# Layer 1's gate with stationary weights, rounded centred sums in linear attention, and a later second pass

## The chip, the cores and the metric

The kernel runs on one core of one Trainium2 chip. The metric is the device time of one launch in microseconds (us). The core has five engines that run their own instruction streams in order: PE (matrix multiplication; its weight loads are shown apart as PEld), DVE, ACT, POOL and SP. They wait for each other by semaphores. Data lies in on-chip SBUF (128 partitions), PE writes into PSUM (8 banks of 128 x 512 f32), and DMA moves data to and from DRAM. Instructions are named as the profile names them: line of the kernel, engine, operation, output tile <- input tiles.

## The reference

The program is a two-layer backbone over 2048 latent tokens and 256 context tokens of width 1024, both of which go through the layers as 18 row tiles of 128 tokens (tiles 0 and 1 are the context). Layer 0 mixes latent attention (8 heads) and bidirectional gated linear attention (4 heads); layer 1 is neighbourhood attention with 16 heads. What the change touches:

```python
# layer 0, gated linear attention: g = log_sigmoid(logits) / 16, forward and backward
b = jnp.cumsum(gi, axis=-2)                       # within a chunk
q_t, k_t = qi * jnp.exp(b), ki * jnp.exp(-b)
o = einsum(q_t, state) + einsum(tril(q_t k_t), vi)
state = state * jnp.exp(b_last) + einsum(ki * jnp.exp(b_last - b), vi)
b = rms_norm(ol_f + flip(ol_b), gla_gain) * silu(zb)
...
# layer 1
q, k, v, z = jnp.split(jnp.dot(h, w_in), 4, axis=-1)      # 1024 columns each
o = neighborhood_attention(rms_norm(q), rms_norm(k), v, k_ctx, v_ctx, rpb)
y = jnp.dot(o * jax.nn.silu(z), w_out)                    # z of the 2048 latent tokens only
```

## The kernel before

**Products.** A projection is made as three matmuls on rounded operands (type f32r): high x high, high x low, low x high, where high is the rounded value and low the rounded rest (`mm3_steps`, L124 to L131). Other products, the sums of `front` and the transposes among them, take plain f32 operands.

**Stages.** `even_latent` and `even_rest` project layer 0. In `even_rest` the gate of latent attention is already projected with the weights stationary: `pair_steps` (L182 to L194) takes 128 columns of weights as the stationary operand and two row tiles (2 x 128 tokens) as the moving one, 256 columns wide, and so gets the gate transposed. `even_mix` runs latent attention (L936 to L1072: 296 steps of two 512-wide score products, two exponentials on ACT and two additions on DVE, L1041) and weaves linear attention (`gla`, L724 to L915) and the splitting of the output weights between its steps. `odd_qk` projects q and k of layer 1; `odd_vz` projects its v (weight blocks 4 and 5) and gate z (blocks 6 and 7) and weaves in the maxima of the attention scores (`maxes`, L1447 to L1502); `odd_attention` does the attention and the output projection.

**Order.** A timeline model at build time fixes the order of the instructions of each engine. `weave` (L133) takes 0.57 steps of `maxes` for each step of the projections; the stream of cells (`stream`, L196) keeps the modulated input of two row tiles in two slots (`ring`, high and low parts) and reloads a slot (`reload`, L372: a 512 KB load into `x`, a rounding on ACT to `hhi`, a subtraction on DVE L380 to `hlo`) when the last cell of its row tile is done.

**Layer 1's gate before.** A cell (row tile t, block j) is 24 matmuls of 512 columns with the input stationary (L129 to L131). For j = 6 and 7 the gate is formed on ACT (tanh) and DVE (L1389), then turned by four f32 transposes on PE (L1429; L1331 for the two cells that `odd_qk` does), copied out of PSUM by ACT and stored to `z1` in runs of 128 tokens.

**Linear attention before.** `front` (L751 to L783) makes the log gates `gG` of one row tile and sums them along the tokens with two f32 matmuls against triangular matrices of 0 and +-1 (L773). `back` makes the products within the tile. `scan` carries the states over the 18 tiles: forwards on POOL, backwards on DVE (L861 to L863). `second` then goes over the tiles again (`enter` L878: add the state's part, L883, square on ACT L885, sum on DVE L887; `leave` L891: normalise, gate, transpose, store). The hook at L1096 takes one step of the second pass or of the weights at every fourth attention step, from the 166th.

Of the kernel before, what the change touches and what calls it, by code (L numbers as in the profile page):

```python
# [17 lines left out]
P = 128  # L18
# [70 lines left out]
class Kern:  # L89
# [634 lines left out]
    def gla(self, gp, gs, g1, gd, pp, tag):  # L724
# [14 lines left out]
        nc.sync.dma_start(tri[:], self.i["tri"])  # L739
        gn = self.tl(gp, [P, 4], "gn")  # L740
# [10 lines left out]
        def front(c):  # L751
# [15 lines left out]
            G = self.tl(g1, [P, 512], "gG", bufs=1)  # L767
            nc.vector.scalar_tensor_tensor(out=G[:], in0=lg[:], scalar=0.0, in1=e[:], op0=ALU.min, op1=ALU.subtract)
            G4 = G[:].rearrange("p (h z d) -> p h z d", z=2, h=H)
            yield  # L770
            mid = bank()
            for z in range(2):
                nc.tensor.matmul(mid[:].rearrange("p (h z d) -> p h z d", z=2, h=H)[:, :, z, :], tri[:, z, :], G4[:, :, z, :], start=True, stop=True)  # L773
            nc.sync.dma_start(self.gE[c, :, 2], G[0::127])
# [103 lines left out]
        def enter(c, qT, oi, zb):  # L878
# [6 lines left out]
            self.act(sq[:], oi[:], AF.Square)  # L885
            ss = self.tl(gs, [P, H], "gss")
            nc.vector.tensor_reduce(out=ss[:], in_=sq[:].rearrange("p (h t) -> p h t", h=H), axis=AX.X, op=ALU.add)  # L887
# [192 lines left out]
    def even_mix(self, e1, win, hT):  # L1080
# [3 lines left out]
        with ExitStack() as es:  # L1084
            with ExitStack() as esa:
# [190 lines left out]
    def odd_qk(self, ws, win, hT):  # L1276
# [7 lines left out]
        with ExitStack() as es:  # L1284
# [7 lines left out]

            def cell(t, j):
                hi, lo = hT[t]
# [4 lines left out]
                for n, _ in enumerate(steps):  # L1299
                    if n == 5 and pend and (len(pend) > 1 or j in (4, 6)):  # L1300
                        fin(*pend.pop(0))
# [4 lines left out]
                if j == 4:  # L1306
# [3 lines left out]
                    return  # L1310
                if j == 6:
                    n = self.tl(sp, [P, 512], "onat", bufs=4)
                    self.gate(n, ps[:].rearrange("p h d -> p (h d)"))
                    self.marks["a"] = self.last_tanh
                    pend.append((t, j, n))
# [11 lines left out]
            def fin(t, j, n):  # L1327
# [5 lines left out]
                if j == 6:  # L1333
                    self.act(hi[:].bitcast(F32), ps[:])
                    nc.gpsimd.dma_start(self.z1[:4, :, (t - NCT) * P : (t - NCT) * P + P].rearrange("j p t -> p j t"), hi[:].bitcast(F32))
                    return
# [40 lines left out]
            cells += [(t, j) for j in (0, 1, 2, 3, 6, 4) for t in (NT - 2, NT - 1)]  # L1377
# [25 lines left out]

    def odd_vz(self, ws, win, hT):
# [3 lines left out]
        with ExitStack() as es:  # L1408
# [6 lines left out]
            def cell(t, j):  # L1415
                hi, lo = hT[t]
                wh, wl = win[j]
                ps = self.tl(pp, [P, 512], "gm")
                yield from self.mm3_steps(ps[:], (lambda k: hi[:, k, :], lambda k: lo[:, k, :]),
                                          (lambda k: wh[:, k, :], lambda k: wl[k][:]), range(KD))  # L1420
                n = self.tl(sp, [P, 512], "ovz", bufs=3)
                if j < 6:
                    self.act(n[:], ps[:])
                    self.store_v(t, j - 4, n)
                    return
                self.gate(n, ps[:])
                pt = self.tl(pp, [P, 4, P], "tp", bufs=1)
                for i in range(4):
                    nc.tensor.transpose(pt[:, i, :], n[:, i * P : i * P + P], self.ident[:])  # L1429
# [3 lines left out]
                (nc.scalar if t >= NCT + 4 else nc.gpsimd).dma_start(self.z1[(j - 6) * 4 : (j - 6) * 4 + 4, :, o : o + P].rearrange("j p t -> p j t"), z[:])  # L1433
# [482 lines left out]
```

## Time and profile before

| | |
|---|---|
| median of 3 runs | 3614.03 us (3608.65 to 3618.55) |
| the profiled execution, its own time | 3613.5 us |
| its span in the trace | 3611.7 us (1.8 us lie around it) |
| instructions in the span | 52299 |
| mean granted clock of PE | 0.987 |
| linear attention: first load (L755), last normalisation (L894) | 1088.7 us, 1831.0 us |
| transposes of the gate in `odd_vz` (L1429): first, last | 2578.4 us, 3009.6 us |

The page gives the busy time of each engine and its share of the span. The windows view gives the same for stretches of time, with the granted clock of PE (1.00 is full) in the column PEclk. The timeline lists instructions by start and duration; a matmul's duration includes its passage through the array, so what a matmul costs PE is read from the distance between two starts. Waits are listed as who waited for whom, with the total, the number and the longest.

### The profile page before, as it was taken

Reading aid. Unit: us, or ns where it says so; the run is one execution under the profiler, and the core shown is the slowest. Engines: PE = TensorE matmul, PEld = TensorE weight load, DVE = VectorE, ACT = ScalarE, POOL = GpSimd, SP = SyncE. Lnnn points to the kernel's source line nnn. Section 1 sums busy time; section 2 is a strip of 40 time slices with the busy share of each in tenths; the row PEclk is TensorE's granted clock in tenths of the full one; section 3 lists DMA queues with packets and bytes.
Section 4 is the critical chain, followed back from the end, with each engine's and each line's share of the span. In section 5 each row is a group of like instructions: output and inputs, shape, how many; then the busy total and the mean of one; then the engine's idle time right before and its main releaser. Section 6 shows DMA issues by size and latency. Waiting matters only on the chain. (4 is left out here: it accounts for less than half of the span.)

```text
span 3611.7 us, 52299 instructions
## 1 busy us (share of the span) xinstructions
PE 3522.7 (98%) x18620; PEld 2751.5 (76%) x18620; DVE 2375.7 (66%) x4876; ACT 1420.3 (39%) x2687; POOL 1210.8 (34%) x1342
## 2 busy tenths in 40 slices
PE   8999999999999999999999999999999999999899
PEld 6888998999986666656657888888788886555577
DVE  4677666888876776697664345455587874777821
ACT  4544551111115555555652134444422222555510
POOL 1433431101011222212312233333444444767743
PEclk9999999999999999999999999999999998999999
DMA  7555463222243342425524554456644438788654
GB/s 253 148 153 161 141 192 110 78 76 89 67 127 74 90 114 66 121 67 145 156 83 146 169 163 129 142 149 193 206 139 124 134 123 206 210 212 218 183 178 153
DMA packets 396687, 513.67 MB, mean 142 GB/s; under 512 B 61230, under 2 KB 275198, under 8 KB 390523
## 3 DMA queue, kind: packets, MB, share of 16 engines
q1 hardware_dynamic: 353242, 418.68, 40.6%
q0 software_dynamic: 20192, 56.97, 5.4%
q10 hardware_dynamic: 22992, 34.68, 2.9%
q8 instruction: 148, 2.42, 0.3%
q14 instruction: 113, 0.92, 0.1%
HBM read 330.61 MB, written 179.59 MB: 141 GB/s over the span
## 5 line engine op out<-in xcount | busy, mean ns | idle before, releaser
L1041 DVE TENSOR_TENSOR acc<-acc,apt 128x512 f32<-128x512 f32 x512 | 377.1, 765 | 150.4 <-ACT apt L106 146.6
L106 ACT ACTIVATE apt<-st 128x512 f32<-128x512 f32 (+1 forms) x592 | 342.9, 593 | 267.2 <-PE st L1052 222.7
L700 DVE TENSOR_REDUCE mm<-mx 128x1 f32<-128x512 f32 (+1 forms) x656 | 390.7, 629 | 81.5 <-PE mx L699 74.6
L992 PE MATMUL av<-apt,av 128*64 128x512 f32 (+1 forms) x1184 | 269.2, 592 | 0.0
L1050 PE MATMUL st<-aq,akh 97*128 97x512 f32 x576 | 246.1, 427 | 0.2 <-ACT apt L106 0.2
L699 PE MATMUL mx<-mk,mq 96*128 96x512 f32 (+1 forms) x656 | 242.7, 372 | 0.0
L106 ACT ACTIVATE u<-gm 128x352 f32<-128x352 f32 (+1 forms) x144 | 70.4, 496 | 436.1 <-PE gm L131 213.9
L1051 PE MATMUL st<-aq,akh 96*128 96x512 f32 x576 | 228.3, 396 | 0.0
L1052 PE MATMUL st<-aq,akl 96*128 96x512 f32 x576 | 227.9, 396 | 0.0
L1484 DVE CUSTOM_DVE_ANT_1 mx<-mx,mtab 128x465 f32<-128x465 f32 (+14 forms) x576 | 184.3, 338 | 48.6 <-PE mx L1478 35.9
L106 ACT ACTIVATE opt<-opt 128x930 f32<-128x930 f32 (+9 forms) x144 | 119.0, 829 | 240.0 <-POOL opt L1782 138.8
L992 PEld LDWEIGHTS av<-apt,av 128*64 128x64 f32 x1184 | 79.8, 136 | 152.1 <-issue 150.0
L1742 DVE TENSOR_TENSOR opt<-st,tab 128x64 f32<-128x64 f32 (+10 forms) x576 | 142.9, 316 | 76.2 <-PE st L1582 46.0
L1617 POOL TENSOR_TENSOR oacc<-oacc,opt 128x682 f32<-128x682 f32 (+9 forms) x144 | 172.6, 1219 | 35.6 <-ACT opt L106 34.2
L1050 PEld LDWEIGHTS st<-aq,akh 97*128 97x128 f32 x576 | 108.6, 188 | 72.4 <-issue 43.4
L1052 PEld LDWEIGHTS st<-aq,akl 96*128 96x128 f32 x576 | 109.7, 190 | 25.2
L699 PEld LDWEIGHTS mx<-mk,mq 96*128 96x128 f32 x656 | 123.7, 189 | 6.0
L1051 PEld LDWEIGHTS st<-aq,akh 96*128 96x128 f32 x576 | 110.2, 191 | 17.6
L106 ACT ACTIVATE x<-px,modB,modA 128x128 f32<-128x128 f32 x272 | 99.1, 468 | 58.4 <-PE px L355 42.6
L1581 PE MATMUL st<-q,kt 128*128 128x480 f32 (+5 forms) x256 | 100.3, 396 | 19.0 <-DVE opt L1742 14.1
L129 PE MATMUL gm<-w0h,hhi 128*128 128x512 f32 x288 | 116.2, 403 | 2.3 <-DVE hhi L367 2.3
L129 PE MATMUL gm<-w1h,hhi 128*128 128x512 f32 x288 | 116.5, 404 | 0.0
(581 smaller groups left out, 10043.8 us busy)
## 6 DMA issues: line engine op xcount, KB each, us to landing
q<-Q SPq DMA_DIRECT2D x48, 512.0 KB
H<-x ACTq DMA_DIRECT2D x36, 512.0 KB
adaw<-ada_w SPq DMA_DIRECT2D x64, 256.0 KB
x<-H SPq DMA_DIRECT2D x32, 512.0 KB
K1t<-okt POOLq DMA_DIRECT2D x32, 512.0 KB, 6.8
kt<-K1t SPq DMA_DIRECT2D x32, 512.0 KB
mtab<-rpb_q SPq DMA_DIRECT2D x16, 899.0 KB
QT<-qkhl SPq DMA_DIRECT2D x36, 384.0 KB
```

Source lines behind the costliest of these rows:

```text
L106: return self.nc.scalar.activation(out, in_, func, **kw)
L129: self.nc.tensor.matmul(out, lh(k), rh(k), start=j == 0, stop=False)
L699: mm = nc.tensor.matmul(ps[:, :w], q[:A_QK, (t % 6) * P : (t % 6) * P + P], k[:A_QK, k0 : k0 + w], start=True, stop=True)
L700: nc.vector.tensor_reduce(out=m[:, t, n : n + 1], in_=ps[:, :w], axis=AX.X, op=ALU.max)
L992: nc.tensor.matmul(O[j, nb][i * 64 : i * 64 + 64, :w], V[j, kt // TT][:, kt % TT, i * 64 : i * 64 + 64], pts[i][:, :w], start=n == 0, stop ...
L1041: self.add = nc.vector.tensor_tensor(out=acc[i][:, :w], in0=a[:, :w], in1=pts[i][:, :w], op=ALU.add)
L1050: nc.tensor.matmul(ps[:, :w], kh[: A_QK + 1, i, kq], qh[: A_QK + 1, :w], start=True, stop=False)
L1051: nc.tensor.matmul(ps[:, :w], kh[:A_QK, i, kq], ql[:A_QK, :w], start=False, stop=False)
L1052: mm = nc.tensor.matmul(ps[:, :w], kl[:A_QK, i, kq], qh[:A_QK, :w], start=False, stop=True)
L1484: nc.vector.tensor_tensor_reduce(out=s, in0=s, in1=tb[:, ri : ri + rn, ci : ci + cn], scale=1.0, scalar=-3e38, op0=ALU.add, op1=ALU.max, a ...
L1617: self.psum = nc.gpsimd.tensor_tensor(out=a, in0=a, in1=pts[:, :, a0 - r0 : a1 - r0, :], op=ALU.add)
L1742: nc.vector.tensor_tensor(out=pt[:, d[0], d[1]], in0=ps[:, d[0], d[1]], in1=tabs[j][i][:, ri : ri + rn, ci : ci + cn], op=ALU.add)
```

## The change

1. `front`: the log gates are written to `e` (f32), rounded by ACT to `gG` (f32r), and the rest `e - gG` goes to a second f32r tile on DVE. The triangular matrices are rounded once into `trr` (0 and +-1 stay what they are). Each of the two f32 matmuls becomes two f32r matmuls (on `gG` and on the rest) that add up in PSUM. The end rows of the log gates are stored from `e`.
2. `enter`: the square on ACT and the sum on DVE become four DVE operations that multiply and sum, one for each head (each is followed by a read of the accumulator).
3. The hook starts at the 174th attention step instead of the 166th.
4. The gate of layer 1: blocks 6 and 7 go through `pair_steps` with two row tiles, in `odd_vz` and for the last two tiles in `odd_qk`. Transposes, their PSUM tile `tp` in `odd_vz` and the copies out of it go; a gate tile is stored in runs of 256 tokens from POOL's queue (`store_z`). The bank of `tp` goes to `mx` (6 instead of 5). The cells of `odd_vz` are in a new order: the gate cells of a pair of tiles (t, t+1) stand between the v cells of t+1 and those of t.

```diff
+        trr = self.tl(gp, [P, 2, P], "trr", F32R, bufs=1)
+        self.act(trr[:], tri[:, :2, :])
...
-            G = self.tl(g1, [P, 512], "gG", bufs=1)
-            nc.vector.scalar_tensor_tensor(out=G[:], in0=lg[:], scalar=0.0, in1=e[:], op0=ALU.min, op1=ALU.subtract)
-            G4 = G[:].rearrange("p (h z d) -> p h z d", z=2, h=H)
+            nc.vector.scalar_tensor_tensor(out=e[:], in0=lg[:], scalar=0.0, in1=e[:], op0=ALU.min, op1=ALU.subtract)
+            nc.sync.dma_start(self.gE[c, :, 2], e[0::127])
+            G = self.tl(g1, [P, 512], "gG", F32R, bufs=1)
+            self.act(G[:], e[:])
+            L = self.tl(gs, [P, 512], "ge", F32R)
+            nc.vector.tensor_tensor(out=L[:], in0=e[:], in1=G[:], op=ALU.subtract)
+            G4, L4 = z4(G[:]), z4(L[:])
             yield
             mid = bank()
             for z in range(2):
-                nc.tensor.matmul(mid[:].rearrange("p (h z d) -> p h z d", z=2, h=H)[:, :, z, :], tri[:, z, :], G4[:, :, z, :], start=True, stop=True)
-            nc.sync.dma_start(self.gE[c, :, 2], G[0::127])
+                nc.tensor.matmul(z4(mid[:])[:, :, z, :], trr[:, z, :], G4[:, :, z, :], start=True, stop=False)
+                nc.tensor.matmul(z4(mid[:])[:, :, z, :], trr[:, z, :], L4[:, :, z, :], start=False, stop=True)
...
-            self.act(sq[:], oi[:], AF.Square)
             ss = self.tl(gs, [P, H], "gss")
-            nc.vector.tensor_reduce(out=ss[:], in_=sq[:].rearrange("p (h t) -> p h t", h=H), axis=AX.X, op=ALU.add)
+            for h in range(H):
+                o = slice(h * P, h * P + P)
+                nc.vector.tensor_tensor_reduce(out=sq[:, o], in0=oi[:, o], in1=oi[:, o], scale=1.0, scalar=0.0,
+                                               op0=ALU.mult, op1=ALU.add, accum_out=ss[:, h : h + 1])
...
-                    if count[0] >= 166 and count[0] % 4 == 2:
+                    if count[0] >= 174 and count[0] % 4 == 2:
...
+            def gated(t, j):
+                wh, wl = win[j]
+                for b in (0, 2):
+                    ps = self.tl(pp, [P, 512], "gm", bufs=3)
+                    for n, _ in enumerate(self.pair_steps(ps, b, (lambda k: wh[:, k, :], lambda k: wl[k][:]))):
+                        if n == 4 and pend:
+                            fin(*pend.pop(0))
+                        if n % 4 == 1 and out_k:
+                            with self.tc.issue_after(self.power.ins):
+                                out_k.pop(0)()
+                        yield
+                    n = self.tl(sp, [P, 512], "onat", bufs=4)
+                    self.gate(n, ps[:])
+                    self.marks["a"] = self.last_tanh
+                    self.store_z(t, (j - 6) * 4 + b, n)
...
-                            pc = self.tl(pp, [P, 2, CTX], "mx", bufs=5)
+                            pc = self.tl(pp, [P, 2, CTX], "mx", bufs=6)
...
+    def store_z(self, t, b, n):
+
+        o = (min(t) - NCT) * P
+        self.nc.gpsimd.dma_start(self.z1[b : b + 2, :, o : o + 256].rearrange("j p t -> p j t"), n[:].rearrange("p (j t) -> p j t", j=2))
...
             def cell(t, j):
+                wh, wl = win[j]
+                w = lambda k: wh[:, k, :], lambda k: wl[k][:]
+                if j > 5:
+                    for b in (0, 2):
+                        ps = self.tl(pp, [P, 512], "gm")
+                        yield from self.pair_steps(ps, b, w)
+                        n = self.tl(sp, [P, 512], "ovz", bufs=3)
+                        self.gate(n, ps[:])
+                        self.store_z(t, (j - 6) * 4 + b, n)
+                    return
...
-                self.gate(n, ps[:])
-                pt = self.tl(pp, [P, 4, P], "tp", bufs=1)
-                for i in range(4):
-                    nc.tensor.transpose(pt[:, i, :], n[:, i * P : i * P + P], self.ident[:])
-                z = self.tl(sp, [P, 4, P], "ozt", bufs=1)
-                self.act(z[:], pt[:])
-                o = (t - NCT) * P
-                (nc.scalar if t >= NCT + 4 else nc.gpsimd).dma_start(self.z1[(j - 6) * 4 : (j - 6) * 4 + 4, :, o : o + P].rearrange("j p t -> p j t"), z[:])
...
-            cells = [(t, j) for j in (7, 5) for t in (NT - 1, NT - 2)]
-            cells += self.cells(list(range(NT))[::-1], (4, 5, 6, 7), lambda t, j: j < 6 or t >= NCT)[8:]
+            cells = [((NT - 1, NT - 2), 7), (NT - 1, 5), (NT - 2, 5)]
+            for t in range(NT - 4, 0, -2):
+                cells += [(t + 1, 4), (t + 1, 5), ((t, t + 1), 6), ((t, t + 1), 7), (t, 4), (t, 5)]
+            cells += [(t, j) for j in (4, 5) for t in (1, 0)]
```

**How the order moves.** PE, the last gate cell before the v cells of the first pair in `odd_vz` (`gm` is the cell's PSUM bank, `w3h` and `w3l` the high and low weights of block 7, `hhi` and `hlo` the input). Before:

```order
L129 MATMUL gm_23572<-w3h_23015,hhi_18332 128x512
L130 MATMUL gm_23572<-w3l_4542_23181,hhi_18332 128x512
L131 MATMUL gm_23572<-w3h_23015,hlo_18333 128x512
L1429 MATMUL tp_23564<-ident_58,ovz_23561 128x128 x4
L129 MATMUL gm_23642<-w1h_23277,hhi_18332 128x512
L130 MATMUL gm_23642<-w1l_4575_23337,hhi_18332 128x512
```

With the change, the same block, where its first pair of 128-column pieces ends and the second begins:

```order
L190 MATMUL gm_23657<-hhi_18460,w3h_23143 128x256
L191 MATMUL gm_23657<-hlo_18461,w3h_23143 128x256
L192 MATMUL gm_23657<-hhi_18460,w3l_4561_23309 128x256
L190 MATMUL gm_23751<-hhi_18460,w3h_23143 128x256
L191 MATMUL gm_23751<-hlo_18461,w3h_23143 128x256
L192 MATMUL gm_23751<-hhi_18460,w3l_4537_23205 128x256
```

The four transposes are gone from between the cells, and the matmuls are half as wide and twice as many.

PE, the sums of the fifth row tile in `front` (`st` is a bank of attention scores, `aq`, `akh` and `akl` their operands, `gl` the bank of linear attention). Before:

```order
L1052 MATMUL st_13197<-aq_13035,akl_10772 128x512
L756 MATMUL gl_11137<-ident_58,gu_1907_11138 96x128
L773 MATMUL gl_11143<-gG_11096,tri_10787 128x4x64 x2
L1050 MATMUL st_13203<-aq_13035,akh_1773_10750 128x512
L1051 MATMUL st_13203<-aq_13035,akh_1773_10750 128x512
```

With the change:

```order
L1060 MATMUL st_13353<-aq_13127,akl_10777 128x512
L779 MATMUL gl_11169<-gG_11120,trr_10789 128x4x64
L780 MATMUL gl_11169<-ge_11122,trr_10789 128x4x64
L779 MATMUL gl_11169<-gG_11120,trr_10789 128x4x64
L780 MATMUL gl_11169<-ge_11122,trr_10789 128x4x64
L822 MATMUL gl_11184<-gqT_11142,gkT_11143 128x128
L1058 MATMUL st_13359<-aq_13127,akh_1774_10751 128x512
```

Two f32 matmuls have become four f32r ones. The whole first pass stands about three attention steps later on PE, and the second pass eight.

DVE, one tile of the second pass. Before (`goi` is the tile's output, `gss` its sums of squares, `acc` the attention's sums):

```order
L883 TENSOR_TENSOR goi_15842<-gl_15929,goi_15842 128x512
L1041 TENSOR_TENSOR acc_3093_15649<-acc_3093_15649,apt_15971 128x512
L887 TENSOR_REDUCE gss_15937<-ge_15935 128x4
L1041 TENSOR_TENSOR acc_3092_15648<-acc_3092_15648,apt_15979 128x512
L1041 TENSOR_TENSOR acc_3093_15649<-acc_3093_15649,apt_15985 128x512
```

With the change:

```order
L889 TENSOR_TENSOR goi_15949<-gl_15953,goi_15949 128x512
L894 ISA ge_15959,gss_15960<-goi_15949 128x128
L894 ISA gss_15960 128x1
L894 ISA ge_15959,gss_15960<-goi_15949 128x128
L894 ISA gss_15960 128x1
L894 ISA ge_15959,gss_15960<-goi_15949 128x128
L894 ISA gss_15960 128x1
L894 ISA ge_15959,gss_15960<-goi_15949 128x128
L894 ISA gss_15960 128x1
L1049 TENSOR_TENSOR acc_3105_15728<-acc_3105_15728,apt_15977 128x512
```

Eight instructions (four products with sums, four reads of the accumulator) stand where one reduction stood, and the attention's addition comes after them.

Up to the first sums of `front`, and from the output projection of layer 0 through `odd_qk` up to its gate cells, the instructions of PE stand in the same order before and after.

More of the change, by code (lines that the diff above doesn't have):

```diff
@@ L1291, in odd_qk @@
             pend, kt, out_k = [], {}, []
+            def gated(t, j):
[13 more added lines that the diff above has]
+                    self.store_z(t, (j - 6) * 4 + b, n)
             def cell(t, j):
+                if j == 6:
+                    yield from gated(t, j)
+                    return
                 hi, lo = hT[t]
@@ L1299, in cell @@
                 for n, _ in enumerate(steps):
-                    if n == 5 and pend and (len(pend) > 1 or j in (4, 6)):
+                    if n == 5 and pend and (len(pend) > 1 or j == 4):
                         fin(*pend.pop(0))
@@ L1309, in cell @@
                     self.store_v(t, 0, n)
[L1310 to L1315, printed above, removed]
                     return
@@ L1376, in odd_qk @@
             cells = self.cells(list(range(NT)), (2, 3, 0, 1), lambda t, j: j > 1 or t >= NCT)[:-8]
-            cells += [(t, j) for j in (0, 1, 2, 3, 6, 4) for t in (NT - 2, NT - 1)]
+            for j in (0, 1, 2, 3, 6, 4):
+                cells += [((NT - 2, NT - 1), j)] if j == 6 else [(t, j) for t in (NT - 2, NT - 1)]
             for _ in self.stream(cells, hT, cell, lambda t: self.prep(1, t, self.x1, pp, ("px", 2)), done):
```

19 lines of the change are left out of this document (6 added, 13 removed).

## The prediction

> **What bounds the kernel now.** I read the page first: the busy shares of the engines and the chain that ended last.
>
> ```profile
> PE 3522.7 (98%) x18620; PEld 2751.5 (76%) x18620; DVE 2375.7 (66%) x4876; ACT 1420.3 (39%) x2687; POOL 1210.8 (34%) x1342
> PE 41%; DVE 2%; DMA 1%; issue 1%; ACT 1%; POOL 0%; SPq 0%; POOLq 0%; DVEq 0%; ACTq 0%
> ```
>
> PE is busy for 98% of the span, no other engine for more than 66%, and of the part of the chain that could be followed PE has by far the most. A share over the whole span hides stages with another limit, so the windows view comes next, for the first pass of linear attention, the end of its scan, its second pass, and `odd_vz`.
>
> ```profile
> core 0: us, PE busy (x) PEld busy (x) DVE busy (x) ACT busy (x) POOL busy (x), PEclk, DMA share, GB/s
> 1070.00:1550.00 480.00, 474.72 (x2428) 303.71 (x2427) 333.53 (x470) 271.81 (x519) 121.79 (x124) 1.00 0.37 94
> 1550.00:1630.00 80.00, 76.51 (x335) 44.59 (x334) 76.21 (x113) 39.42 (x67) 6.68 (x5) 0.98 0.26 72
> 1640.00:1840.00 200.00, 200.00 (x975) 126.49 (x975) 139.46 (x219) 123.23 (x261) 60.52 (x59) 1.00 0.53 149
> 2570.00:3010.00 440.00, 431.70 (x2104) 360.61 (x2103) 335.25 (x1362) 113.08 (x187) 187.85 (x162) 0.99 0.43 134
> ```
>
> PE is the limit in all four. DVE comes close in one: 76.2 of 80 us at the end of the scan, where PE loses 3.5 us. The waits of PE, in 1070 to 1900 us (first row) and in 2540 to 3060 us (the others), are few:
>
> ```profile
> PE gl L825 <- DVE gat L821: 3.5, 1, 3.5
> ...
> PE mx L1478 <- DVE mm L1473: 3.2, 2, 3.0
> PE mx L1471 <- DMA mk<-K: 2.0, 1, 2.0
> PE mx L1478 <- DVE mm L1484: 1.6, 2, 1.0
> PE tp L1429 <- DVE ovz L1389: 1.4, 1, 1.4
> ```
>
> So the time is set by what PE is given to do, and the change is costed as PE work, with the other engines as a check.
>
> **Transposes removed.** The timeline of PE near the end of `odd_vz` shows a run of 512-column matmuls and then one group of four transposes.
>
> ```profile
> 3000.46 0.40 PE L129 MATMUL gm<-w3h,hhi 128*128 128x512 f32 x1
> ...
> 3002.77 0.39 PE L130 MATMUL gm<-w3l,hhi 128*128 128x512 f32 x1
> 3003.00 0.60 PE L1429 MATMUL tp<-ident,ovz 128*128 128x128 f32 x4
> 3003.35 0.48 PE L131 MATMUL gm<-w3h,hlo 128*128 128x512 f32 x1
> 3003.67 0.40 PE L129 MATMUL gm<-w0h,hhi 128*128 128x512 f32 x1
> ```
>
> From 3000.46 to 3002.77 there are ten starts: 0.231 us for one matmul of 512 columns. From 3002.77 to 3003.67 PE did two of these (0.462) and the group: 0.90 - 0.462 = 0.44 us for the group, the slow first matmul behind it included. The number of groups:
>
> ```profile
> L1429 PE MATMUL tp<-ident,ovz x120: 270/272/328, 2578.4 to 3009.6; 128*128 128x128 f32 x120
> ```
>
> That is 30 groups, and the two gate cells of `odd_qk` have one each. 32 x 0.44 = **14.1 us less**.
>
> **Matmuls of half the width.** Two cells of 24 matmuls x 512 columns become 96 x 256. The gate in `even_rest` already runs in this form:
>
> ```profile
> L190 PEld LDWEIGHTS gm<-hhi,WUh x288: 187/190/193, 545.0 to 1063.8; 128*128 128x128 f32 x144
> 545.21 0.28 PE L190 MATMUL gm<-hhi,WUh 128*128 128x256 f32 x1
> ...
> 556.21 0.28 PE L190 MATMUL gm<-hhi,WUh 128*128 128x256 f32 x1
> ```
>
> Between the two starts lie 93 matmuls: 11.00 / 93 = 0.1183 us each. A pair of cells costs 96 x 0.1183 = 11.36 us against 48 x 0.231 = 11.09, so 0.27 more, and 16 pairs (16 row tiles, two blocks) **4.3 us more**. The weight loads last 0.19 us each, longer than the distance of the matmuls, and are hidden all the same, since successive ones overlap. In the Trainium skill, "TensorE: Matmul & The Clock Gate" (part 1, on the measured gap) a warm matmul has a fixed cost of about 2.5 ns beside its columns. By that figure the 768 additional matmuls would cost 1.9 us, as an estimate. The rows here decide: they give 4.3 us.
>
> **Sums of `front`.** One row tile of the first pass:
>
> ```profile
> 1183.53 0.40 PE L1052 MATMUL st<-aq,akl 96*128 96x512 f32 x1
> 1183.77 1.03 PE L773 MATMUL gl<-gG,tri 128*128 128x256 f32 x4
> 1184.44 0.58 PE L1050 MATMUL st<-aq,akh 97*128 97x512 f32 x1
> 1184.87 0.40 PE L1051 MATMUL st<-aq,akh 96*128 96x512 f32 x1
> ```
>
> The two f32 products (four records) take 0.67 us, and the next matmul 0.43 instead of 0.23 to 0.24. From 1183.77 to 1184.87 is 1.10 us with one matmul in it. After the change four rounded matmuls of 256 columns and that one take 4 x 0.118 + 0.235 = 0.71. The difference is 0.39 us, x 18 tiles **7.0 us less**. The trace has no rounded matmul whose columns come in pieces of 64; the bounds are 0.20 x 18 = 3.6 us (0.67 - 0.47, the slow successor stays, as where an f32 product follows) and 9 us (0.03 us more for each weight load that then runs ahead); I take 7.0, which the rows give directly.
>
> The sum on PE: -14.1 + 4.3 - 7.0 = **-16.8 us**.
>
> **What goes to other engines.**
>
> ```profile
> L768 DVE SCALAR_TENSOR_TENSOR gG<-gl,ge 128x512 f32<-128x512 f32 x18 | 12.3, 686 | 3.5 <-ACT ge L106 3.3
> L887 DVE TENSOR_REDUCE gss<-ge x18: 677/680/686, 1641.6 to 1828.2; 128x4 f32<-128x512 f32 x18
> L1484 DVE DVE_READ_ACCUMULATOR2_ANT mm<- 128x1 f32 x576 | 82.4, 144 | 0.0
> L1484 DVE CUSTOM_DVE_ANT_1 mx<-mx,mtab 128x120 f32<-128x120 f32 x32 | 9.4, 294 | 0.3 <-PE mx L1478 0.3
> L106 ACT ACTIVATE ovz<-gm 128x512 f32<-128x512 f32 x62 | 36.8, 594 | 113.7 <-PE gm L131 98.5 <-DVE mm L1473 6.1 <-DVE mm L1484 4.8
> ```
>
> In `front` DVE gets a subtraction of the size of L768, 0.69 x 18 = 12.3 us, and ACT a copy of 0.59 x 18 = 10.7. DVE goes from 333.5 to 346 of 480 us; PE hides it. The chain from the log gate to its sums grows by 0.69 + 0.59 = 1.3 us, and the order gives the first pass some three attention steps for it. In `enter` DVE loses 0.68 and gets four times 0.294 + 0.144, together 1.75: +1.07 x 18 = 19.3 us, so that DVE is busy 159 of 200 us instead of 139.5, still under PE. ACT loses 18 squares, and in the gate 32 copies of 0.594. All of this I cost at nothing. Without PE's cover it would be up to 12.3 + 19.3 = 31.6 us. Queued behind the four sums on DVE are the attention's additions, and for those the buffers of ACT's exponentials; the stretch 1550 to 1630 shows DVE 95% busy with PE losing 3.5 us in one place only, so 80% does not reach PE.
>
> **Second pass eight steps later.**
>
> ```profile
> L862 DVE TENSOR_TENSOR gsb<-gsb,D x17: 687/689/690, 1162.9 to 1628.6; 64x512 f32<-64x512 f32 x17
> L883 DVE TENSOR_TENSOR goi<-gl,goi x18: 691/692/694, 1639.6 to 1826.2; 128x512 f32<-128x512 f32 x18
> ```
>
> The scan ends on DVE at about 1630 us and the second pass starts 10 us later. It has 17 x 4 = 68 steps from 1639.6 to 1826.2, 2.74 us each, so the delay is about 22 us. The scan is about three steps (8 us) later, which leaves it a gap of 24 instead of 10 us. The same work moves to later attention steps, in which PE is full anyway: cost nothing. What is late then is the split of the last output weights; 27 steps are left before the last block of attention, as many as there are calls. The wait at L825 (3.5 us) may go or stay: 0, with -5 and +4 as its bounds (the idle time and the lower clock that follows it).
>
> **Reloads and stores in `odd_vz`.** Between the release of a slot and the next use of its tile lay at least four cells in the middle of the stage, and now two: 2 x 24 x 0.231 = 11.1 us, more with the maxima between. The work in it:
>
> ```profile
> L380 DVE TENSOR_TENSOR hlo<-x,hhi x32: 1214/1220/6297, 568.8 to 3004.3; 128x1024 fp32r<-128x1024 f32 x32
> L106 ACT ACTIVATE hhi<-x x13: 1044/1060/1063, 2625.0 to 2975.8; 128x1024 fp32r<-128x1024 f32 x13
> L1433 POOL DMA_DIRECT2D z<-ozt x8: 772/796/816, 2918.7 to 3014.0; - x8
> ```
>
> 1.06 + 1.22 = 2.3 us, once 7.4 us with the longest subtraction: it fits. 22 of the 30 stores of `odd_vz` move from ACT's to POOL's queue, where two more cells add two: 24 x 0.8 = 19 us on an engine that is busy 188 of 440 us, whose mask additions run a head ahead. One more bank for `mx` may save part of the 4.8 us that PE waited for DVE; the first pair cells get the maxima closer together, which may cost 3. Together 0, from -5 to +6.
>
> **The sum.** The profiled execution took 3613.5 us (span 3611.7 and 1.8 around it), 0.5 under the median of the runs. 3613.5 - 16.8 = 3596.7; beside the median 3614.0 it is **3597 us**.
>
> **The rivals.**
>
> (a) DVE sets `odd_vz`. It is busy 335 of 440 us there and its waits show up as three of PE's four. If the maxima take back what the gate frees, only the 7.0 us of `front` are left: 3607. Against it: PE's waits there sum up to 8 us, and a sixth bank loosens that tie.
>
> (b) New stalls at the gate cells: slower. A pair cell cannot start before both tiles are in their slots, so a late reload stops PE. What such a stop costs is shown by the one of 3.0 us between 2640 and 2680:
>
> ```profile
> 2640.00:2680.00 40.00, 37.02 (x176) 30.72 (x175) 32.39 (x127) 8.75 (x15) 13.82 (x13) 0.96 0.43 136
> ```
>
> 3.0 us idle and 0.04 x 40 = 1.6 us by the lower clock: 4.6. One at each of the seven pairs is 32 us: 3613.5 - 16.8 + 32 = 3629. It decides from four stops on. For it: slack falls from four cells to two, and one L380 took 6.3 us. Against it: 11.1 us are there for 2.3.
>
> (c) The scan's end becomes a DVE stretch. The 12.3 us of `front` and a later scan add to the place that is 95% busy; if all 12.3 reach PE, 3609. Against it: only the last two tiles' subtractions lie near the scan.
>
> (d) The sums do not get faster (pieces of 64 columns at half rate): 3604.
>
> (e) The weight loads set the pace. If each matmul of 256 columns took the 0.19 us of its weight load, 1536 x 0.07 = 108 us more: about 3705. The rows of L190 speak against it, at 0.1183. The same page of the Trainium skill (back-to-back issue gap) gives 81 ns for 128 columns and 131 ns for 512 in a stream with weight loads, by which halving the columns saves little of a matmul; the rows of this case differ, with 0.231 for 512.
>
> **How the numbers follow.** The forecast has 0.72, (a) 0.12, (b) 0.05, (c) 0.05, (d) 0.05, (e) 0.01. Its own range comes from the bounds: -5 and +6 in `odd_vz`, -5 and +4 at the scan, -2 and +3.4 in `front`, not all at once: 3589 to 3604. To hold 8 in 10 the range reaches up to (a) and (d): 3589 to 3607. A measurement of this kernel tells about 0.3% (10.8 us) from no change, so faster means under 3603.2. Nearly all of the forecast lies there (0.70); its rest, (a), (c) and (d) are no change (0.23); (b), (e) and what I have not seen are slower (0.07).
>
> **What would show it.** In the changed profile: no transposes in `odd_vz`, and the stage some 10 us shorter at about the same DVE work; starts of 256-column gate matmuls 0.118 us apart; the four matmuls of `front` about 0.47 us together with the next matmul at 0.235; DVE about 159 of 200 us in the second pass with PE at 200. It is wrong if PE shows new waits for `hhi` or `hlo` at the gate cells, for DVE at the end of the scan, or for the rounded rest before its sums, beyond some 6 us.

## The result, and the profile after

The changed kernel takes **3580.42 us** (median of 4 runs, 3576.06 to 3587.56) beside 3612.54 us of the kernel before on the same chip (3608.65 to 3618.55): a ratio of 0.9912 with a 95% interval of 0.9890 to 0.9933, 32 us less. The forecast was 3597 us with a range of 3589 to 3607: the direction was right, the gain was nearly twice as large. The profiled execution of the changed kernel took 3587.56 us, the longest of its four, with a granted clock of 0.988 over the span where the other three had 0.991.

The page of the changed kernel, busy time by engine and shares of the chain that ended last:

```profile
PE 3499.2 (98%) x19260; PEld 2764.4 (77%) x19260; DVE 2380.5 (66%) x5020; ACT 1404.5 (39%) x2656; POOL 1221.8 (34%) x1364
PE 86%; DVE 4%; DMA 4%; ACT 2%; issue 2%; POOL 2%; SPq 0%; POOLq 0%; DVEq 0%; ACTq 0%
```

PE still sets the time. To see where the time went, the span is cut at three places whose work is the same in both kernels. The tile views give first and last starts (durations min/median/max in ns ahead of them); first the kernel before:

```profile
L648 POOL DMA_DIRECT2D zaT<-u x18: 715/727/733, 559.5 to 1066.3; - x18
L129 PE MATMUL pj<-gu,prh x32: 389/394/501, 1940.4 to 2109.3; 128*128 128x512 f32 x32
L355 PE MATMUL px<-ident,x x272: 270/272/477, 8.2 to 2500.2; 128*128 128x128 f32 x136
L1582 PE MATMUL st<-q,kt x256: 282/328/522, 3038.9 to 3419.0; 65*128 65x360 f32 x32, 65*128 65x480 f32 x32, 65*128 65x288 f32 x16, 65*128 65x384 f32 x16
L1581 PE MATMUL st<-q,kc x128: 392/399/793, 3026.2 to 3393.5; 128*128 128x512 f32 x128
```

And the same five rows of the changed kernel:

```profile
L648 POOL DMA_DIRECT2D zaT<-u x18: 715/727/733, 563.1 to 1071.2; - x18
L129 PE MATMUL pj<-gu,prh x32: 389/395/628, 1936.5 to 2107.6; 128*128 128x512 f32 x32
L355 PE MATMUL px<-ident,x x272: 270/272/476, 8.5 to 2498.8; 128*128 128x128 f32 x136
L1605 PE MATMUL st<-q,kt x256: 282/328/458, 3013.6 to 3390.6; 65*128 65x360 f32 x32, 65*128 65x480 f32 x32, 65*128 65x288 f32 x16, 65*128 65x384 f32 x16
L1604 PE MATMUL st<-q,kc x128: 392/399/504, 3009.5 to 3364.8; 128*128 128x512 f32 x128
```

Stage A is `even_mix` (last store of `zaT` to first `pj`), stage B `odd_vz` with the end of `odd_qk` (last transpose `px` to the first context score `st<-q,kc`), stage C the neighbourhood attention (that score to the last `st<-q,kt`).

| | before | after | difference | forecast |
|---|---|---|---|---|
| A | 874.1 | 865.3 | -8.8 | -7.0 |
| B | 526.0 | 510.7 | -15.3 | -9.8 |
| C | 392.8 | 381.1 | -11.7 | 0 |
| the rest | 1818.8 | 1828.7 | +9.9 | 0 |

The sum is -25.9, as the spans have it (3611.7 to 3585.8). The rest is code that the change does not touch. Most of its 9.9 us is time that differs from one execution to the next: over all thirteen profiled kernels of this study the last store of `zaT` starts between 1066.3 and 1073.3 us. But 2.5 us of it are not: from the last `st<-q,kt` to the end there are 192.7 to 193.6 us in the four kernels without part 4 and 195.2 to 196.5 in the nine with it. The difference lies behind the last matmul, which starts 7.0 us before the end in the kernel before and 9.2 us in the changed one; its cause stays open. Stage C, 11.7 us, stands in no term of the forecast.

### The profile page after: what moved, and what is told of

It is laid out like the page before. It is cut to its first block, busy times and chain, and to the rows that moved or that the text cites. A ratio compares the mean times of both kernels' runs of the same rounds, so it can differ in the third digit from the quotient of the medians.

```text
span 3585.8 us, 53487 instructions
## 1 busy us (share of the span) xinstructions
PE 3499.2 (98%) x19260; PEld 2764.4 (77%) x19260; DVE 2380.5 (66%) x5020; ACT 1404.5 (39%) x2656; POOL 1221.8 (34%) x1364
## 4 chain that ended last, share of the span: by engine, by line
PE 86%; DVE 4%; DMA 4%; ACT 2%; issue 2%; POOL 2%; SPq 0%; POOLq 0%; DVEq 0%; ACTq 0%
PE gm L131 8%; PE gm L129 8%; PE gm L130 8%; PE av L1000 7%; PE st L1058 4%; PE mx L699 4%; PE st L1060 3%; PE st L1059 3%; PE gm L190 2%; PE gm L191 2%; PE gm L192 2%; PE o L1634 2%; PE st L1604 2%; PE st L129 2%; PE st L131 2%; PE st L130 2%
## 5 line engine op out<-in xcount | busy, mean ns | idle before, releaser
L1505 DVE CUSTOM_DVE_ANT_1 mx<-mx,mtab 128x465 f32<-128x465 f32 (+12 forms) x576 | 180.1, 342 | 28.6 <-PE mx L1499 23.0
L106 ACT ACTIVATE x<-px,modB,modA 128x128 f32<-128x128 f32 x272 | 99.3, 468 | 58.3 <-PE px L355 48.3
L131 PE MATMUL gm<-w0h,hlo 128*128 128x512 f32 x288 | 115.1, 400 | 5.0 <-DVE hlo L380 4.9
```

What stands on the lines that cost most here:

```text
L106: return self.nc.scalar.activation(out, in_, func, **kw)
L131: yield self.nc.tensor.matmul(out, ll(k), rh(k), start=False, stop=j == n - 1)
L1505: nc.vector.tensor_tensor_reduce(out=s, in0=s, in1=tb[:, ri : ri + rn, ci : ci + cn], scale=1.0, scalar=-3e38, op0=ALU.add, op1=ALU.max, a ...
```

## Where the gain in the attention comes from

The windows of the first 40 us of stage C, before and after (PEclk is the granted clock):

```profile
3026.20:3066.20 40.00, 33.86 (x159) 22.03 (x159) 17.62 (x48) 15.64 (x26) 21.54 (x13) 0.74 1.05 274
```

```profile
3009.50:3049.50 40.00, 38.91 (x262) 25.19 (x261) 22.07 (x74) 21.62 (x34) 28.02 (x23) 1.00 0.92 225
```

Busy time by clock, an estimate, PE did 33.86 x 0.74 = 25.1 us of work before and 38.9 after. What was late shows in the waits of POOL, PE and SP's queue around 3000 us, before:

```profile
POOL tab L1574 <- DMA q<-maskk: 15.1, 1, 15.1
...
PE st L1581 <- ACT opt L106: 5.7, 1, 5.7
...
SPq L111 <- PE mx L1478: 21.8, 1, 21.8
```

SP's queue has a load standing for 21.8 us until the last maxima matmul (L1478, at 3000.33) has been done: the new stage's tiles lie where those of the maxima were. In SP's timeline the first loads for the attention start right then; before:

```profile
3000.66 1.77 SPq L111 DMA_DIRECT2D q<-Q  x3
```

and after:

```profile
2967.05 1.80 SPq L111 DMA_DIRECT2D q<-Q  x3
```

From the first load to the first score there are 25.5 us before and 42.5 after. PE's wait of 5.7 us is for the exponentials of the first context scores. ACT's timeline shows what they stand behind; before:

```profile
3026.43 0.60 ACT L106 ACTIVATE ovz<-gm 128x512 f32<-128x512 f32 x1 [4.89 <-PE gm L131]
3032.94 0.33 ACTq L1398 DMA_DIRECT2D V1c<-ovz  x1
3033.31 2.56 ACT L106 ACTIVATE opt<-st 128x512 f32<-128x512 f32 x5 [6.29 <-DMA kt<-K1t]
```

and after:

```profile
3009.70 0.60 ACT L106 ACTIVATE ovz<-gm 128x512 f32<-128x512 f32 x1 [4.89 <-PE gm L131]
3010.33 0.34 ACTq L1416 DMA_DIRECT2D V1c<-ovz  x1
3010.72 4.03 ACT L106 ACTIVATE opt<-st 128x512 f32<-128x512 f32 x8 [0.42 <-PE st L1605]
```

The exponentials (`opt<-st`) stand behind the last store of `odd_vz` (`V1c`) in ACT's queue. Its tile is ready at 3027.03, but before it was issued 5.9 us later, by the profile when a load of keys (`kt<-K1t`) had landed, one of the late loads of the new stage; after, it is issued at once. Why this store waits for that load the profile does not say. POOL's 15.1 us for the mask are not on this path: context scores take no mask, POOL's additions of it end at 3035.56, and the first operation of DVE that reads them, at 3039.46, came when PE's scores were there.

The new order of cells had put 43.0 us of projections (95232 columns at 0.231 us per 512) behind the last maxima matmul, instead of 24.9 (55296 columns). **Theory:** this lead, from the end of the maxima to the first score, makes the hand-over from one stage to the next clean and so pays for stage C. **Rivals:** chance, or the linear attention's new order.

## The experiments

All medians are beside runs of the kernel before on the same chip; A, B and C are read in each profile as above. They stand together here.

| kernel | median us | ratio, 95% interval | A | B | C |
|---|---|---|---|---|---|
| gate_only | 3589.16 | 0.9931, 0.9916 to 0.9945 | 873.8 | 510.2 | 377.7 |
| sums_only | 3613.64 | 0.9999, 0.9989 to 1.0010 | 874.3 | 519.6 | 394.8 |
| before_r60 | 3595.98 | 0.9951, 0.9935 to 0.9967 | 873.9 | 519.9 | 380.9 |
| after_r54 | 3593.36 | 0.9939, 0.9925 to 0.9953 | 866.3 | 511.2 | 386.5 |
| after_166 | 3582.12 | 0.9923, 0.9910 to 0.9936 | 871.5 | 509.9 | 378.2 |
| after_square | 3584.64 | 0.9919, 0.9906 to 0.9933 | 865.5 | 510.2 | 381.7 |
| after_mx5 | 3580.81 | 0.9913, 0.9899 to 0.9926 | 865.5 | 510.4 | 376.8 |
| after_mask2 | 3578.91 | 0.9908, 0.9895 to 0.9922 | 868.0 | 502.4 | 379.0 |
| sums_174 | 3604.05 | 0.9982, 0.9971 to 0.9993 | 866.3 | 524.8 | 391.3 |
| after_r60 | 3589.45 | 0.9939, 0.9926 to 0.9953 | 866.7 | 512.7 | 381.6 |
| after_mask2_r60 | 3575.31 | 0.9903, 0.9890 to 0.9916 | 866.2 | 503.7 | 377.7 |

**The hand-over: before_r60 and after_r54.** One number each, no work added or removed:

```diff
-            self.weave(gemms, maxes(), 0.57, 15)
+            self.weave(gemms, maxes(), 0.60, 15)
```

for before_r60, in the kernel before, and

```diff
-            self.weave(gemms, maxes(), 0.57, 15)
+            self.weave(gemms, maxes(), 0.54, 15)
```

for after_r54, in the changed kernel.

> The kernel before with one number changed: 0.60 instead of 0.57 steps of the maxima to a step of the projections, so that 41.6 us of projections stand behind the last maxima matmul instead of 24.9. No instruction is added or removed. Theory (hand-over): POOL's wait for the mask goes, PE's wait of 5.7 us at the first local scores goes and the clock stays at 1.00 there: 8 to 12 us less, 3601 to 3605 us. Rival 1 (the hand-over does not depend on when the maxima end): no change, 3612 us. Rival 2 (denser maxima make PE wait for DVE): slower, 3615 us or more, although the hand-over is clean.

> The changed kernel with one number changed: 0.54 instead of 0.57 steps of the maxima to a step of the projections, so that 25.6 us of projections stand behind the last maxima matmul, as in the kernel before (24.9), instead of 43.0. Theory (hand-over): POOL waits for the mask and PE at the first local scores again, attention is 8 to 12 us longer: 3588 to 3592 us. Rival (the gain in attention comes from elsewhere): no change, 3580 us, or a little faster since the maxima press less on DVE.

The kernel before gets 3595.98 us, 17.6 us less. The changed kernel gets 3593.36, 13 us more in the median (10 by the two ratios, whose intervals just overlap). The first 40 us of stage C, before_r60 first, then after_r54:

```profile
3024.10:3064.10 40.00, 38.90 (x262) 25.29 (x260) 22.11 (x75) 21.54 (x34) 28.06 (x23) 1.00 0.91 225
```

```profile
3009.20:3049.20 40.00, 33.69 (x194) 21.75 (x192) 24.68 (x56) 17.53 (x28) 27.61 (x20) 0.91 1.06 264
```

In before_r60 the stretch takes the form of the changed kernel's, and PE's wait of 5.7 us is gone. In after_r54 it goes only part of the way: PE is busy for as little as in the kernel before, but at a clock of 0.91 and not 0.74. The store ahead of the exponentials is 1.5 us late instead of 5.9, and the longest wait of PE is 2.9 us, for DVE. Its C is 5.4 us longer than that of the changed kernel, less than the 8 to 12 us expected; the rest of its loss is in no stage. In the table C is 376.8 to 381.7 in all nine with 41.6 us or more behind the last maxima, and 386.5 to 394.8 in all four with about 25. The theory holds in both directions, in its full size only in the kernel before. That before_r60 won more than the 12 us of C is its B, 6 us shorter; but sums_only, with the same work in B, has the same 519.6, so this is the spread of B in the kernels with transposes (519.6 to 526.0).

**The parts apart: gate_only, sums_only, sums_174.** The kernel before with part 4 alone, of whose diff these lines are the new order:

```diff
+            for t in range(NT - 4, 0, -2):
+                cells += [(t + 1, 4), (t + 1, 5), ((t, t + 1), 6), ((t, t + 1), 7), (t, 4), (t, 5)]
```

with part 1 alone (sums_only; its core):

```diff
+                nc.tensor.matmul(z4(mid[:])[:, :, z, :], trr[:, z, :], G4[:, :, z, :], start=True, stop=False)
+                nc.tensor.matmul(z4(mid[:])[:, :, z, :], trr[:, z, :], L4[:, :, z, :], start=False, stop=True)
```

and with part 1 and part 3 (sums_174):

```diff
-                    if count[0] >= 166 and count[0] % 4 == 2:
+                    if count[0] >= 174 and count[0] % 4 == 2:
```

> The kernel before with part 4 alone (the gate of layer 1 with stationary weights and its new order of cells, 6 banks for the maxima); sums, second pass and its start are as before. As in the changed kernel, 43.0 us of projections stand behind the last maxima matmul in PE's order, and 24.9 us in the kernel before. Theory (hand-over): the maxima end earlier, so the loads of the neighbourhood attention land before it begins; odd_vz gets about 15 us shorter, and the attention about 12 us: 27 us in all, about 3586 us against 3612.5. Rival 1 (the 12 us in the attention were chance or came with the linear attention's later order): only odd_vz is shorter, about 3598 us. Rival 2 (the transposes are worth no more than forecast, 14.1 - 4.3): about 3603 us.

> The kernel before with part 1 alone (rounded sums in front); the order of odd_vz and its end are as before. Theory: linear attention's stretch 7 to 9 us shorter, nothing else: 3604 to 3606 us. Rival (pieces of 64 columns run at half rate, or DVE takes it back): within 3 us of the kernel before, 3610 to 3613 us. The hand-over keeps its wait of some 15 us on POOL for the mask.

> The kernel before with part 1 (rounded sums) and part 3 (the hook at the 174th attention step) alone: the squares stay on ACT, odd_vz and its end are as before. Theory (the sums save 8 us and the later start keeps them): linear attention's stretch is 865 to 867 us instead of 874, no wait of 5 us of PE for the exponentials at the start of the second pass, 3603 to 3606 us beside 3611 to 3613 of the kernel before. Rival (the square on ACT stalls the exponentials wherever the second pass starts): as the sums alone, within 2 us of the kernel before.

gate_only has B and C of the changed kernel and A of the kernel before, 24.4 us less: three quarters of the change. sums_only gains nothing, against theory: A is 874.3. Its trace has a new wait at the start of the second pass; the wait of ACT there, and PE's timeline:

```profile
ACT ge L106 <- DVE goi L889: 5.5, 1, 5.5
```

```profile
1639.66 0.40 PE L1058 MATMUL st<-aq,akl 96*128 96x512 f32 x1
1645.31 0.80 PE L1056 MATMUL st<-aq,akh 97*128 97x512 f32 x1 [5.25 <-ACT apt L106]
1645.90 0.63 PE L1057 MATMUL st<-aq,akh 96*128 96x512 f32 x1
...
1650.73 1.56 PE L929 MATMUL den<-acc,mtwos 128*64 128x512 f32 x4
```

and DVE's timeline just before, with the last step of the scan and the first addition of the second pass:

```profile
1642.70 0.69 DVE L869 TENSOR_TENSOR D<-gsb,fac 64x512 f32<-64x512 f32 x1
1643.42 0.69 DVE L889 TENSOR_TENSOR goi<-gl,goi 128x512 f32<-128x512 f32 x1
```

Here the scan ends right before the addition, where the kernel before had 8 us between them (L863 ends at 1631.4, L883 starts at 1639.6). Measured from the last store of `zaT` the scan ends 6.4 us later than before and the addition starts 1.8 us earlier. The first pass already begins 8.4 us later (first copy, L808 and L814, at 58.3 and 66.7 us), as its new place in the order has it; whether the 18 subtractions on DVE make it later still, no run shows. The square (`ge`) stands in ACT's queue and waits 5.5 us for it, the exponentials stand behind the square, and PE waits 5.25 us for them. Then its matmuls start 0.43 us apart instead of 0.23, to 1650.73: some twelve at 0.2 us more, 2.4 us. Together 7.7 us, what the sums had saved. With the hook eight steps later the wait is gone and A is 866.3 (sums_174, 3604.05 us): the later start keeps the gain.

**Which of parts 2 and 3 is needed: after_166 and after_square.** Each takes one of them out of the changed kernel; after_166 part 3,

```diff
-                    if count[0] >= 174 and count[0] % 4 == 2:
+                    if count[0] >= 166 and count[0] % 4 == 2:
```

and after_square part 2:

```diff
+            self.act(sq[:], oi[:], AF.Square)
...
-            for h in range(H):
-                o = slice(h * P, h * P + P)
-                nc.vector.tensor_tensor_reduce(out=sq[:, o], in0=oi[:, o], in1=oi[:, o], scale=1.0, scalar=0.0,
-                                               op0=ALU.mult, op1=ALU.add, accum_out=ss[:, h : h + 1])
+            nc.vector.tensor_reduce(out=ss[:], in_=sq[:].rearrange("p (h t) -> p h t", h=H), axis=AX.X, op=ALU.add)
```

> The changed kernel with the hook at the 166th attention step, as before; the squares stay on DVE. With the rounded sums alone ACT waited 5.5 us for the first addition of the second pass, with the exponentials behind it, and PE 5.25 us for these, then at a lower clock: about 8 us, as much as the sums had saved. Theory 1 (the square on ACT is what holds the exponentials): with the square on DVE no such stall, 3580 to 3583 us. Theory 2 (the start of the second pass while the scan is late is what costs, whoever squares): the stall returns, about 3588 us.

> The changed kernel with the square on ACT and one sum on DVE, as before; the hook stays at the 174th step. Theory 1 (the square on ACT is what holds the exponentials): if the addition that it waits for is still late after 22 us, the stall returns, about 3588 us. Theory 2 (the later start is what helps): the scan ends well before the second pass begins, no stall, 3578 to 3581 us, and DVE is 19 us less busy.

Without part 2 stage A stays at 865.5, as expected: with the later start the square on DVE brings nothing. Without part 3 it is 871.5, so 6 of the 8.8 us go, and no wait of 5 us shows: the square on DVE spares the exponentials, and the early start costs in another form, of which the list of waits has one of 2.3 us of PE for a later step of the second pass; the rest of the 6 us was not followed up. The medians, 1.7 and 4.2 us above that of the change (the second above the expected 3578 to 3581 us), lie within the spread of its runs; the stages decide here.

**The sixth bank: after_mx5.** `bufs=6` becomes 5 in the three tiles of `mx`.

> The changed kernel with 5 instead of 6 banks for the maxima (one bank unused). Theory: the sixth bank is worth little, since in PE's order 42.4 us of projections stand behind the last maxima matmul with 5 banks and 43.0 with 6, and the hand-over stays clean: 3580 to 3584 us. Rival (the waits of 7 us of PE on DVE's maxima, which the changed kernel lost, went by the sixth bank): 3586 to 3590 us, with these waits in the list again.

3580.81 us, and B 510.4: the bank is worth nothing. The waits of PE on the maxima did not come back, so they went with the rest of part 4.

**A new stop that was found in stage B: after_mask2.** PE's waits from 2510 to 3100 us in the changed kernel, in the form of those shown before:

```profile
PE gm L131 <- DVE hlo L380: 4.9, 1, 4.9
PE gm L129 <- DVE ovz L1407: 2.1, 1, 2.1
...
PE mx L1492 <- DMA mk<-K: 0.8, 1, 0.8
PE mx L1492 <- DVE mm L1505: 0.6, 1, 0.6
```

The waits on the maxima (3.2 and 1.6 us before) are all but gone, and there is one for `hlo` at the first reload. A smaller new one, for the gate on DVE (L1407), is in all nine kernels with part 4 (1.6 to 3.1 us) and was not followed up. The subtraction in DVE's timeline, and the masks of the maxima in POOL's:

```profile
2588.51 10.26 DVE L380 TENSOR_TENSOR hlo<-x,hhi 128x1024 fp32r<-128x1024 f32 x1 [6.09 <-ACT hhi L106]
```

```profile
2586.09 3.22 POOL L1477 TENSOR_TENSOR mtab<-mtab,maskq 128x1798 f32<-128x1798 f32 x1
2589.25 3.74 POOL L1478 TENSOR_TENSOR mtab<-mtab,maskq 128x1798 f32<-128x1798 f32 x1
2592.91 1.09 POOL L1420 DMA_DIRECT2D V<-ovz  x2
2594.01 3.67 POOL L1478 TENSOR_TENSOR mtab<-mtab,maskq 128x1798 f32<-128x1798 f32 x1
```

10.26 us instead of 1.22, and it ends 1.1 us after the last of the three additions, as if it had only begun there. Subtractions of 3.1 to 6.3 us stand beside such additions at other reloads, before and after, and PE waited for none of them. In the Trainium skill, "SBUF — State Buffer" (SBUF: two separate sides) says that DVE with two operands in SBUF and a GpSimd operation that reads SBUF take a shared pair of ports as a lock, for a whole instruction, and that the loser is fully blocked. By that rule moving the additions away frees the subtraction. The edit, made in the same way for the second addition (L1478):

```diff
-                    nc.gpsimd.tensor_tensor(out=tb[:], in0=tb[:], in1=mk[:, :NR].unsqueeze(2).to_broadcast([P, NR, NC]), op=ALU.add)
+                    (nc.vector if h < 2 else nc.gpsimd).tensor_tensor(out=tb[:], in0=tb[:], in1=mk[:, :NR].unsqueeze(2).to_broadcast([P, NR, NC]), op=ALU.add)
```

> The changed kernel with the additions of the mask for the first two heads of the maxima on DVE instead of POOL (four operations of 128x1798). In the changed kernel the first reload's subtraction on DVE took 10.26 us instead of 1.22, beside these additions on POOL, and PE waited 4.9 us for it, the stretch 2560 to 2600 having PE busy for 32.2 of 40 us at a clock of 0.91. Theory (the two engines hold each other up there): the subtraction takes 1.2 us again, the wait goes, 5 to 8 us less: 3572 to 3576 us. Rival (the subtraction waits for its input, the length is only how it shows; or the additions on DVE delay it as much): 3580 us or more.

In its DVE timeline an addition of the mask and the subtraction read

```profile
2588.03 2.03 DVE L1477 TENSOR_TENSOR mtab<-mtab,maskq 128x1798 f32<-128x1798 f32 x1
...
2590.72 1.23 DVE L380 TENSOR_TENSOR hlo<-x,hhi 128x1024 fp32r<-128x1024 f32 x1
```

1.23 us again; the wait for `hlo` is gone, and B is 502.4, 8.3 us shorter. The windows of 2560 to 2600 us tell why it is more than the 4.9 us of the wait: the clock is higher too, 0.96 instead of 0.91. The changed kernel, then after_mask2:

```profile
2560.00:2600.00 40.00, 32.22 (x183) 28.20 (x182) 16.45 (x25) 5.35 (x9) 18.34 (x12) 0.91 0.61 207
```

```profile
2560.00:2600.00 40.00, 37.86 (x212) 32.93 (x211) 20.95 (x51) 7.26 (x11) 6.16 (x11) 0.96 0.72 236
```

The trace thus agrees with that rule of the Trainium skill. The median, 3578.91, misses the expected 3572 to 3576: it is only 1.5 us below that of the change, under what these runs can tell apart, though the stage shows the gain.

**More lead: after_r60 and after_mask2_r60.** The changed kernel and after_mask2, with 0.60 instead of 0.57 in the line of `weave`.

> The changed kernel with 0.60 instead of 0.57 steps of the maxima to a step of the projections: 55.7 us instead of 43.0 of projections behind the last maxima matmul. Theory (the hand-over is paid once the loads are in before the attention begins, and they are already): no further gain, 3577 to 3583 us. Rival 1 (each us of lead still counts): 3570 to 3576 us. Rival 2 (denser maxima make PE wait for DVE): 3584 us or more.

> The changed kernel with the mask of the first two heads of the maxima on DVE, and 0.60 instead of 0.57. With the mask alone the stretch of odd_vz was 8 us shorter in the profiled execution, and the median 2 to 4 us lower than that of its neighbours. Theory (the two are independent, the second worth nothing): 3574 to 3580 us, odd_vz at 502 us. Rival (the 8 us are given back in the attention): 3580 us or more.

A longer lead, 55.7 us, brings C nothing (381.6 and 377.7 us, within those with 43.0). So there is a threshold and not a price by the microsecond; it lies between leads of 25.6 and 41.6 us, and none between them was tried. after_r60 came out at 3589.45, as rival 2 has it, but its B is only 2.0 us longer and PE's waits for DVE's maxima 1.7 us; the rest of the 9 us isn't explained by a stage, and after_mask2_r60, equally dense, is the fastest kernel of the study: **3575.31 us** (3572.30 to 3577.42), 37 us below the kernel before. It beats the change by 5 us in the median; the intervals of the two ratios overlap.

## Why the prediction was half right

- **What bounds the kernel.** Right: PE, with 98% of the span as before.
- **Transposes, -14.1.** Right as far as it can be told: with the new stop taken out (after_mask2), B is 502.4 and 503.7, against 519.6 to 526.0 in the four kernels with transposes. That is 16 to 24 us: the 14.1, and PE's shorter waits in this stage (5 to 8.5 us in those four by their lists, 2 to 3 in these two). In the changed kernel itself PE waits as long as before (8.4 and 8.2 us), and B is 15.3 us shorter.
- **Half width, +4.3.** The mechanism was right (the weight loads stay hidden), the size was not: the term measured about 1 us. PE's timeline of the changed kernel, the last matmuls of 512 columns and a stretch of 256:

```profile
2560.00 0.39 PE L131 MATMUL gm<-w0h,hlo 128*128 128x512 f32 x1
...
2564.81 0.39 PE L131 MATMUL gm<-w0h,hlo 128*128 128x512 f32 x1
...
2565.51 0.28 PE L191 MATMUL gm<-hlo,w3h 128*128 128x256 f32 x1
...
2575.72 0.28 PE L191 MATMUL gm<-hlo,w3h 128*128 128x256 f32 x1
```

  21 intervals of 0.2290 us, and 90 of 0.1134: two halves take 0.2268. Over all of `odd_vz`, with maxima between, successive halves start 0.1160 us apart (mean of 1276 intervals) and successive matmuls of 512 columns 0.2307 (607). Two halves then cost 1.3 ns more than the whole, and the 768 of them 1.0 us. In the Trainium skill, "TensorE: Matmul & The Clock Gate" (part 1, on the measured gap) has a fixed cost of 2.5 ns for each matmul; the rows shown have none, and the means of the stage about half of it. The 0.118 had come from another stage, in which DMA was 98% busy. The first seven halves of the changed kernel, up to 2565.75, start 0.118 us apart too, and the next ones 0.113; whether DMA is the reason was not tried.
- **Sums, -7.0.** Right in size: sums_174 saves 7.8 us in A, the whole change 8.8. On PE the sums of the 18 tiles, each with the matmul behind it, take 22.6 us before and 15.1 after, 7.5 less; four of them take 0.48 us (1194.17 to 1194.65), as forecast.
- **"Second pass eight steps later ... cost nothing".** As a cost it was right, as a part it was misjudged: the forecast let the sums pay by themselves, and by themselves they pay nothing (sums_only). It costed DVE's and ACT's additions at nothing because PE had cover on average; the place that has none is the scan's end, where ACT's square waits in front of the exponentials. Rival (c) named the place, and the later start was what kept it from happening. The gap there became 17 us in the changed kernel, not 24. The products and sums on DVE were priced too high: one tile's take 0.93 us (1656.26 to 1657.19) and not 1.75, and over 188.6 us of the second pass DVE is busy 4.7 us longer (137.6 after, 132.9 before) and not 19.3.
- **"Reloads and stores in `odd_vz` ... Together 0, from -5 to +6".** The one long new stop, rival (b)'s kind, cost 8 us, outside the range, for a DVE subtraction behind POOL's masks that took more than the slack had room for; at the seven later pairs there is none. It was made up for by the waits on the maxima that went with the new order (PE's waits in all: 8.2 us before, 8.4 after). The bank was worth 0.
- **The step that failed:** the sum ended at the last gate cell. The change moves the end of the maxima 18 us forward against the projections, as the order shows, and what waits for that end, the loads of the next stage, was not asked for. The trace of before had it in plain sight (21.8 us of SP's queue until the last maxima, 5.7 of PE, a clock of 0.74 over the 40 us). The runs showed 12 us in its place (11.7 in the change, 11.9 in before_r60): most of the 17 us by which the forecast fell short. The half-width term, 4.3 instead of about 1, is another 3; the remaining 2 are less than the runs can tell apart.

## What to carry to other kernels

When a change moves the end of a side stream, ask what the next stage loads into the space that it frees: a hand-over can be worth nearly as much as the work removed (here 12 us of C beside 15 of B), and one number in the weave gets it without any work removed. A saving on the engine that bounds is only kept if the work that pays for it on another engine isn't late at the one place without slack, so look at in-order queues behind a late input (here exponentials behind a square), not at busy shares. Price a matmul's form from rows in the stage where it will run.

## What the runs showed of the hardware that was not expected

- A stop of PE costs more than its length: in sums_only 5.25 us of waiting cost 7.7, with the matmuls behind it 0.43 us apart instead of 0.23, and the late start of the attention had a mean granted clock of 0.74 over 40 us.
- The clock also drops without a stop that would tell why: the second 40-us piece of stage C has PE busy for 38.82 us at 0.96 in the changed kernel and 38.73 us at 1.00 in after_mx5. A clock of 0.988 or 0.991 over the span goes with 3587.6 or 3576 to 3581 us of one and the same kernel.
- A DVE subtraction of 1.22 us took 10.26 beside three POOL additions in a row, and did not end between them, not even in the 1.0 us in which POOL only issued a store. Another, of 3.14 us at 2882.66, did: it ended at 2885.80 in such a pause, as the next addition started.
